# Up products of two feed-forward layers: wide matmuls on high and low parts side by side, then narrow ones

## The chip, the cores and the metric

One core of a Trainium2 chip. The metric is the time of the kernel on the device in microseconds (us), as the median of several runs. All times are for one launch with the inputs of the reference.

## The reference, cut to what matters

A block of a language model, for 512 tokens of width 1024, in float32: a gated feed-forward layer, a mixer (a short convolution and gated linear attention), a second gated feed-forward layer, and a last norm.

```python
def swiglu(x, w_gu, w_down):
    g, u = jnp.split(x @ w_gu, 2, axis=-1)      # 1024 -> 2 x 2816: the "up" products
    return (jax.nn.silu(g) * u) @ w_down        # 2816 -> 1024: the "down" products

x = x + 0.5 * swiglu(rmsnorm(x, norm_ffn1_g), ffn1_w_gu, ffn1_w_down)
x = x + hybrid_mixer(rmsnorm(x, norm_mix_g), ...)
x = x + 0.5 * swiglu(rmsnorm(x, norm_ffn2_g), ffn2_w_gu, ffn2_w_down)
return rmsnorm(x, final_norm_g)
```

## The kernel before, in words

**Layout and precision.** x stands transposed (`X`: 128 partitions, 8 blocks of the width, 512 tokens). A matmul of the kernel takes operands of 128 partitions in the type float32r, which keeps fewer bits than float32. So each operand is split into a high part (ScalarE rounds it: a cast) and a low part (VectorE subtracts the high part), and each product is the sum of three: high by high, high by low, low by high. ScalarE and VectorE split the weights as they arrive (`Weights.issue`, lines 331 and 332: `wh` and `wl`, three buffers each, made up to two products ahead); `Operands.make` (lines 561 and 562) does it for x.

**Sets.** Most of the up products are made in sets by a scheme of seven products in place of eight (as Strassen's): a set makes two column blocks of 256 of the gate and two of the up half, from seven products of sums of weight blocks with sums of x blocks. The products are named m1, p2, q6, p5, q7, p4, p3. The sums of the weights are made by VectorE (line 318, `s3`) and by DMAs that add (line 309, issued on GpSimd's queue); loads are issued on SyncE's queue some steps ahead. The sums of x are made in place (`Operands.sum`, lines 543 to 548), once per layer and during its first set. Each of the seven results goes into one of three accumulators of the set, `a`, `b` or `c`; a PSUM bank holds 512 float32 values a partition, and an accumulator is one bank: two blocks of 128 output columns by 256 tokens. The products of two following sets are interleaved by `order`: ... q6, p5, q7 of a set, m1 of the next, p4, p2 of the next, p3, and then q6 of the next. After the first set m1 is also copied into the next `a` ("fork", line 507).

A product in `Set.run` (line 502) is 24 matmuls, each with its own 128x128 weight tile and 256 columns of x: eight of high weights by high x, eight of high by low x, eight of low by high x. After m1, q6 and q7 ScalarE copies the bank to SBUF (`v`); the rest is done by the function `done` of `up_set` (lines 720 to 745): SiLU of the gate straight from bank `a` after p2, then combinations by VectorE, into the hidden tiles `h`.

**Banks.** There are eight PSUM banks: a pool of six (`MM`) and a pool of two (`AUX`).

**A feed-forward layer** (`ffn`, from line 648): first a "plain" stage without sets for four of the 22 blocks (`mm_group`, `mm_single`, `plain_pair`: VectorE multiplies each bank by the row of the norm, line 476), then nine sets, then the down products: two wide sets of seven products in matmuls of 512 columns (`natural_set`, line 625; `run_wide`), each product in two steps of 12 matmuls, the first three being m1, p5 and q6; then the rest (line 838). In the second layer x has to be turned for the end, since the result leaves with tokens on partitions: `natural(i)` (lines 771 and 772) turns one of eight blocks with four TensorE transposes into an `AUX` bank, and ScalarE copies it back. It is called after p3 of the sets 0 to 7.

Which engine an instruction runs on is fixed in the code. The order of an engine's queue comes from a planner that keeps, by its own estimate of times, to the order of the program where it can and pulls later instructions forward where an engine would be idle.

Of the kernel before, what the change touches and what calls it, by code (L numbers as in the profile page):

```python
# [8 lines left out]
F32 = mybir.dt.float32  # L9
F32R = mybir.dt.float32r  # L10
# [5 lines left out]
P = 128  # L16
# [163 lines left out]
def block_kernel(ctx: ExitStack, tc: tile.TileContext, xT, vecs, gf, gup, wgl, wts, out):  # L180
# [6 lines left out]
    ps = ctx.enter_context(tc.tile_pool(name="ps", bufs=6, space=bass.MemoryType.PSUM))  # L187
    pa = ctx.enter_context(tc.tile_pool(name="pa", bufs=2, space=bass.MemoryType.PSUM))

    cnt = [0]  # L190

# [14 lines left out]
    def T(dtype=F32):  # L206
        return tile_of("tp", [P, S], dtype)

    def MM():
        cnt[0] += 1  # L210
        return ps.tile([P, S], F32, tag="mm", name=f"mm{cnt[0]}")

    def AUX():
        cnt[0] += 1
        return pa.tile([P, S], F32, tag="aux", name=f"aux{cnt[0]}")


    ones = front.tile([P, P], F32, tag="ones", name="ones")
# [260 lines left out]
    class Set:  # L479
# [34 lines left out]
        def first(self):  # L514
# [4 lines left out]
            nc.vector.tensor_tensor(out=t, in0=self.bank["a"], in1=self.v["m1"], op=ALU.add)  # L519
            return t  # L520

    class Operands:

        ORDER = ("m1", "p2", "p5", "q6", "q7", "p4", "p3")

        def __init__(self, b):
            self.b = b
            self.parts = {}  # L530
            self.sums = set()

# [19 lines left out]
        def make(self, p):  # L552
            if p in self.parts:
                return
            i = self.ORDER.index(p)
            if i > 0:
                self.make(self.ORDER[i - 1])
            v = self.sum(p)
            h, l = (tile_of("op", [P, 1024], F32R) for _ in range(2))
            hv, lv = (t.rearrange("p (k t) -> p k t", t=HW) for t in (h, l))  # L560
            nc.scalar.copy(hv, v)
            nc.vector.tensor_tensor(out=lv, in0=v, in1=hv.bitcast(F32), op=ALU.subtract)
            self.parts[p] = (h, l)
# [40 lines left out]
        def get(self, p):  # L604
            return self.parts[p]

    def natural_set(ops, banks, done, ahead=1):

        used = {"a"}
        for at, p in enumerate(SEQ):  # L610
            for q in SEQ[at : at + ahead + 1]:
                ops.make(q)
            n = {"m1": "b", "p2": "a", "q6": "b", "p5": "c", "q7": "b", "p4": "b", "p3": "c"}[p]
            fresh = n not in used
            used.add(n)
            o = banks[n]
            bh, bl = ops.get(p)
            for u in range(2):
                h, l = W.take()
                for j, (ww, aa) in enumerate(((h, bh), (h, bl), (l, bh))):  # L620
                    for i in range(2):
                        k = 2 * u + i
                        for t in range(2):
                            s = slice(k * HW + t * P, k * HW + (t + 1) * P)
                            nc.tensor.matmul(o[t], aa[:, s], ww[:, i * 512 : (i + 1) * 512],  # L625
                                             start=fresh and j == k == 0,
                                             stop=j == 2 and k == 3, skip_group_check=True)
            done(p, o)

    def run_sets(make, ahead=2, hooks={}):  # L630
# [19 lines left out]
    def ffn(up, down, norm, nxt, plain, at):  # L650
        xh, xl = norm.h, norm.l
        rows = []

        def finish(k):
            if k == at:
                rows.append(norm.finish())

        o = mm_group(up, KD, (0, DFF, P, DFF + P), xh, xl, extra=finish, slow=nxt is not None)
        row = rows[0]
        xn, xn_tile = {}, []  # L660

        def normed(j, l):

            if (j, l) not in xn:
                t = slice(l * HW, (l + 1) * HW)
                if not xn:
                    xn_tile.append(tile_of("hidw", [P, 4, 4, HW]))
                v = xn_tile[0][:, len(xn)]
                for i in range(4):
                    k = 4 * j + i  # L670
                    nc.vector.scalar_tensor_tensor(
                        out=v[:, i], in0=x[k][:, t],
                        scalar=vec[:, norm.goff + k : norm.goff + k + 1], in1=row[:, t],
                        op0=ALU.mult, op1=ALU.mult)
                xn[j, l] = v
            return xn[j, l]

        xo = Operands(normed)
# [36 lines left out]

        def down_operands(w):
            return DownOperands(
                lambda j, l: wides[w][:, 4 * j : 4 * j + 4, l * HW : (l + 1) * HW])

        def up_set(i):  # L720
            h = new_hid()

            def done(s, p):
                bank, v = s.bank, s.v
                if p == "p2":
                    s.g1 = T()
                    nc.scalar.activation(s.g1, s.first(), AF.Silu)
                if p == "q7":
                    u2 = T()
                    nc.vector.scalar_tensor_tensor(out=u2, in0=bank["c"], scalar=-1.0, in1=v["q7"],  # L730
                                                   op0=ALU.mult, op1=ALU.subtract)
                    s.u2 = u2
                if p == "p4":
                    nc.vector.scalar_tensor_tensor(
                        out=h[:, :, :HW], in0=pair(bank["b"]), scalar=-1.0, in1=pair(s.g1),
                        op0=ALU.mult, op1=ALU.mult)
                if p == "p3":
                    g2 = T()
                    nc.vector.tensor_tensor(out=g2, in0=bank["c"], in1=v["q6"], op=ALU.add)
# [9 lines left out]
            return Set(xo, done)  # L749

        def pair(t):
            return t.rearrange("p (e t) -> p e t", t=HW)

        run_sets(up_set)

        def split_hid(k):
# [17 lines left out]
    def down_product(us, split_hid, downs, nxt):  # L774
# [26 lines left out]
        A = [MM(), MM()]  # L801

        def run_wide(w):
            banks = {"a": A, "b": [(MM, AUX)[w % 2]() for _ in range(2)], "c": [MM(), MM()]}

            def done(p, o):
                for t in range(2):
# [12 lines left out]

            natural_set(downs[w], banks, done)
            return banks["c"]

        for w in range(WIDE):
            C = run_wide(w)
# [728 lines left out]
```

## Time and profile before

| | |
|---|---|
| median of 3 runs | 1181.12 us (1181.11 to 1181.16) |
| the profiled execution | 1180.99 us, span 1179.3 us |
| TensorE (PE) busy | 1170.9 us, 99% |
| VectorE (DVE) busy | 868.9 us, 74% |
| ScalarE (ACT) busy | 634.3 us, 54% |
| GpSimd (POOL) busy | 117.4 us, 10% |
| matmuls in sets, high weights / low weights | 3584 / 1792 |

A group of instructions is named by its line, engine and operation, and by its output and input (`mm<-op,wh`: into a bank from an operand of x and high weights). Matmuls are pipelined: the busy time of one is longer than the distance to the next, so their distance is read from the start of a run of them and their count. The chain is the work that ended last, followed back from the end, here in order of time: start, length, engine, tile, line, count. In brackets behind an instruction stands how long its engine was idle before it and what released it. In a full queue an instruction starts some 0.1 us before the end that is shown for the one ahead of it.

### The profile page before, as it was taken

How to read it: one execution, taken by the hardware profiler on the slowest of the kernel's cores; microseconds unless marked ns; L12 is line 12 of the kernel's file. 1: busy time of each engine (PE TensorE's matmuls, PEld its weight loads, DVE VectorE, ACT ScalarE, POOL GpSimd, SP SyncE). 2: the span in 40 equal slices, each digit the busy share in tenths (PEclk: the TensorE clock that was granted, in tenths of full speed). 3: DMA queues.
4: the chain of work that ended last, by engine and by line, in shares of the span. 5: the costliest groups of instructions: out<-in, count | busy, mean ns of one | idle time of the engine just before them, and what ended most of it. 6: DMA issues, size and time to landing. Idle time of an engine off the chain costs nothing.

```text
span 1179.3 us, 19168 instructions
## 1 busy us (share of the span) xinstructions
PE 1170.9 (99%) x7794; PEld 1080.7 (92%) x7794; DVE 868.9 (74%) x1027; ACT 634.3 (54%) x790; POOL 117.4 (10%) x153
## 2 busy tenths in 40 slices
PE   9999999999999999999999999999999999999997
PEld 8899999988888889999999998998889999998886
DVE  7985656896568965767697787685598566579955
ACT  6564455674435655565565576544355554566543
POOL 0010101101010111100110100000001111001100
PEclk9999999999999999999999999999999999999999
DMA  9388777678524388777677766531638767757721
GB/s 350 79 210 197 171 193 178 158 199 206 212 85 113 87 207 223 189 180 200 180 196 192 199 199 186 141 109 44 232 68 211 181 180 175 190 153 186 178 83 72
DMA packets 62600, 200.25 MB, mean 170 GB/s; under 512 B 6864, under 2 KB 13136, under 8 KB 62512
## 3 DMA queue, kind: packets, MB, share of 16 engines
q0 software_dynamic: 18784, 68.17, 31.7%
q1 hardware_dynamic: 39088, 126.37, 30.9%
q10 hardware_dynamic: 4640, 4.49, 1.1%
q8 instruction: 61, 1.00, 0.3%
q14 instruction: 27, 0.22, 0.1%
HBM read 124.55 MB, written 8.39 MB: 113 GB/s over the span
## 4 chain that ended last, share of the span: by engine, by line
PE 97%; ACT 1%; issue 1%; DVE 1%; ACTq 0%; POOL 0%; POOLq 0%
PE mm L502 53%; PE mm L625 12%; PE mm L366 11%; PE mm L380 7%; PE mm L838 4%; PE aux L625 4%; PE aux L838 1%; PE aux L1161 1%; PE aux L1142 1%; PE aux L1120 1%; PE aux L1164 0%; PE aux L224 0%; PE aux L1121 0%; PE mm L857 0%; PE aux L771 0%
## 5 line engine op out<-in xcount | busy, mean ns | idle before, releaser
L331 ACT CAST wh<-f 128x1024 fp32r<-128x1024 f32 (+1 forms) x341 | 356.2, 1047 | 406.3 <-PE mm L502 207.4
L332 DVE TENSOR_TENSOR wl<-f,wh 128x1024 fp32r<-128x1024 f32 (+1 forms) x341 | 413.3, 1217 | 154.1 <-ACT wh L331 141.3
L502 PE MATMUL mm<-op,wh 128*128 128x256 f32 x3584 | 471.1, 284 | 0.4 <-ACT mm L507 0.4
L502 PEld LDWEIGHTS mm<-op,wh 128*128 128x128 f32 x3584 | 447.9, 192 | 2.2 <-ACT mm L507 0.8
L502 PE MATMUL mm<-op,wl 128*128 128x256 f32 x1792 | 251.5, 283 | 0.0
L502 PEld LDWEIGHTS mm<-op,wl 128*128 128x128 f32 x1792 | 231.2, 192 | 0.1
L309 POOL DMA_DIRECT2D f<-f x126 | 108.9, 869 | 929.0 <-DVE wl L332 542.2
L625 PE MATMUL mm<-wh,op 128*128 128x512 f32 x432 | 106.9, 389 | 0.0
L625 PEld LDWEIGHTS mm<-wh,op 128*128 128x128 f32 x432 | 80.9, 188 | 16.7
L366 PE MATMUL mm<-op,wh 128*128 128x512 f32 x384 | 91.0, 389 | 0.0
L366 PEld LDWEIGHTS mm<-op,wh 128*128 128x128 f32 x384 | 72.0, 188 | 14.9
L380 PE MATMUL mm<-op,wh 128*128 128x512 f32 x256 | 64.2, 393 | 0.0
L625 PE MATMUL mm<-wl,op 128*128 128x512 f32 x216 | 57.7, 389 | 0.0
L380 PEld LDWEIGHTS mm<-op,wh 128*128 128x128 f32 x256 | 48.1, 189 | 10.3
L318 DVE TENSOR_TENSOR f<-f,f 128x1024 f32<-128x1024 f32 x42 | 51.3, 1222 | 0.8
L625 PEld LDWEIGHTS mm<-wl,op 128*128 128x128 f32 x216 | 40.6, 188 | 8.4
L366 PE MATMUL mm<-op,wl 128*128 128x512 f32 x192 | 47.4, 389 | 0.0
L366 PEld LDWEIGHTS mm<-op,wl 128*128 128x128 f32 x192 | 36.0, 188 | 7.5
L510 ACT COPY tp<-mm 128x512 f32<-128x512 f32 x68 | 39.6, 583 | 0.0
L601 DVE TENSOR_TENSOR op<-hidw,op 128x1024 fp32r<-128x1024 f32 x28 | 34.0, 1219 | 1.1 <-ACT op L600 1.0
L380 PE MATMUL mm<-op,wl 128*128 128x512 f32 x128 | 34.3, 389 | 0.0
L416 ACT ACTIVATE op<-X,vec 128x512 fp32r<-128x512 f32 x23 | 16.5, 719 | 31.8 <-DVE X L859 24.3
(269 smaller groups left out, 1042.5 us busy)
## 6 DMA issues: line engine op xcount, KB each, us to landing
f<-wts SPq DMA_DIRECT2D x219, 512.0 KB, 4.5
f<-f POOLq DMA_DIRECT2D x126, 512.0 KB, 5.3
X<-xT SPq DMA_DIRECT2D x8, 256.0 KB, 5.3
xs<-X POOLq DMA_DIRECT2D x8, 256.0 KB, 2.3
ga<-tp ACTq DMA_DIRECT2D x8, 256.0 KB, 3.2
gb<-tp ACTq DMA_DIRECT2D x8, 256.0 KB, 4.7
tp<-ga SPq DMA_DIRECT2D x8, 256.0 KB, 4.3
y<-tp SPq DMA_DIRECT2D x7, 256.0 KB, 2.3
```

Of the source, the lines that this page charges most:

```text
L309: return nc.gpsimd.dma_start(out_, a, accum_op=ALU.add).ins
L318: nc.vector.tensor_tensor(out=s3, in0=a11, in1=a21, op=ALU.add)
L331: self.cast = nc.scalar.copy(h[:, :w], raw[:, :w]).ins
L332: nc.vector.tensor_tensor(out=l[:, :w], in0=raw[:, :w], in1=h[:, :w].bitcast(F32), op=ALU.subtract)
L366: nc.tensor.matmul(o, w[:, i * P : (i + 1) * P], a[k], start=j == k == 0, stop=j == 2 and k == kt - 1)
L380: nc.tensor.matmul(o[c], w[:, s : s + P], a[k], start=k == 0 and j == 0, stop=k == kt - 1 and j == 2)
L416: nc.scalar.activation(xh[k], x[k], AF.Copy, scale=g)
L502: nc.tensor.matmul(to, ww[:, s], aa[:, t], start=fresh and k == 0 and e == 0 and j == 0, stop=k == 3 and j == 2, skip_group_check=True)
L510: nc.scalar.copy(v, o)
L601: nc.vector.tensor_tensor(out=lv, in0=v, in1=hv.bitcast(F32), op=ALU.subtract)
L625: nc.tensor.matmul(o[t], aa[:, s], ww[:, i * 512 : (i + 1) * 512], start=fresh and j == k == 0, stop=j == 2 and k == 3, skip_group_check=True)
L838: nc.tensor.matmul(o[t][e], b if j == 1 else a, wl if j == 2 else wh, start=k == K0 and e == 1 and j == 0, stop=k == KF - 1 and j == 2, sk ...
```

## The change

1. x's parts of an up product are made by a new class `Both`: two tiles, each with high and low part side by side for two of the four blocks. The split of a product's x is two copies and two subtractions of 512 elements in place of one each of 1024.
2. `PairSet` takes the place of `Set` in `up_set` of both layers (the mixer keeps `Set`). An accumulator is two banks, one for each block of 128 output columns; each has the sums with high x on its left and high by low on its right. A product is eight matmuls of 512 columns (high weights by high and low x), then eight of 256 (low weights by high x, onto the left half). Order of sets and products is as before.
3. Since the result is left plus right, evictions change: `taken` (after m1, q6, q7) is two copies by ScalarE and an addition by VectorE; `whole` is a copy and an addition; `both` is two additions. The fork copies two banks.
4. The eight banks: during the sets one pool with four accumulators of two banks (`w`, `x`, `y`, `z`); `a` is always `x`, and `b` and `c` rotate over the others. The pools of six and two are opened again behind the sets.
5. The eight `natural(i)` of the second layer move from the sets into the first wide set of its down products: two after each of its first two steps, then one after each of the next four. The addition into x after p5 is held until the end of q6.

```diff
+    def banks(paired=False):
+        stage.close()
+        for n, b in (("pairs", 1),) if paired else (("mm", 6), ("aux", 2)):
+            cnt[0] += 1
+            pools[n] = stage.enter_context(tc.tile_pool(
+                name=f"{n}{cnt[0]}", bufs=b, space=bass.MemoryType.PSUM, reuse_waits="tile"))
...
+    def MM2(tag):
+        cnt[0] += 1
+        return pools["pairs"].tile([P, 2, S], F32, tag=tag, name=f"{tag}_{cnt[0]}")
...
+    class Both:
+        def __init__(self, v):
+            self.t = []
+            for i in range(2):
+                t = tile_of("op", [P, 2, 2, HW], F32R)
+                w = v[:, 2 * i : 2 * i + 2]
+                nc.scalar.copy(t[:, :, 0], w)
+                nc.vector.tensor_tensor(out=t[:, :, 1], in0=w, in1=t[:, :, 0].bitcast(F32),
+                                        op=ALU.subtract)
+                self.t.append(t)
...
+    class PairSet:
+        BANK = {"m1": "b", "p2": "a", "q6": "b", "p5": "c", "q7": "b", "p4": "b", "p3": "c"}
+        def __init__(self, group_, done, i):
...
+            self.tags = {"a": "x", "b": "wzy"[i % 3], "c": "ywz"[i % 3]}
...
+        def run(self, p):
+            n = self.BANK[p]
+            fresh = n not in self.bank
+            o = self.open(n) if fresh else self.bank[n]
+            x_ = self.group.get(p)
+            h, l = W.take()
+            for k in range(4):
+                for e in range(2):
+                    nc.tensor.matmul(o[:, e], h[:, k * HW + e * P : k * HW + (e + 1) * P],
+                                     x_.both(k), start=fresh and k == 0, stop=False,
+                                     skip_group_check=True)
+            for k in range(4):
+                for e in range(2):
+                    nc.tensor.matmul(o[:, e, :HW], l[:, k * HW + e * P : k * HW + (e + 1) * P],
+                                     x_.high(k), start=False, stop=k == 3,
+                                     skip_group_check=True)
+            if p == "m1" and self.forked:
+                nc.scalar.copy(self.open("a"), o)
+            elif p in ("m1", "q6", "q7"):
+                self.taken(p, n)
+            self.done(self, p)
+        def taken(self, p, n):
+            v, r = T(), T()
+            nc.scalar.copy(pair(v), self.left(n))
+            nc.scalar.copy(pair(r), self.right(n))
+            nc.vector.tensor_tensor(out=v, in0=v, in1=r, op=ALU.add)
+            setattr(self, p, v)
+        def both(self, n, t):
+            for part in (self.left(n), self.right(n)):
+                nc.vector.tensor_tensor(out=pair(t), in0=part, in1=pair(t), op=ALU.add)
+        def whole(self, n):
+            t = T()
+            nc.scalar.copy(pair(t), self.right(n))
+            nc.vector.tensor_tensor(out=pair(t), in0=self.left(n), in1=pair(t), op=ALU.add)
+            return t
...
             def done(s, p):
-                bank, v = s.bank, s.v
                 if p == "p2":
-                    s.g1 = T()
-                    nc.scalar.activation(s.g1, s.first(), AF.Silu)
+                    if s.forked:
+                        s.g1 = s.whole("a")
+                    else:
+                        s.g1 = s.m1
+                        s.both("a", s.g1)
+                    nc.scalar.activation(s.g1, s.g1, AF.Silu)
                 if p == "q7":
-                    u2 = T()
-                    nc.vector.scalar_tensor_tensor(out=u2, in0=bank["c"], scalar=-1.0, in1=v["q7"],
-                                                   op0=ALU.mult, op1=ALU.subtract)
-                    s.u2 = u2
+                    s.both("c", s.q7)
                 if p == "p4":
+                    t = s.whole("b")
                     nc.vector.scalar_tensor_tensor(
-                        out=h[:, :, :HW], in0=pair(bank["b"]), scalar=-1.0, in1=pair(s.g1),
+                        out=h[:, :, :HW], in0=pair(t), scalar=-1.0, in1=pair(s.g1),
                         op0=ALU.mult, op1=ALU.mult)
                 if p == "p3":
-                    g2 = T()
-                    nc.vector.tensor_tensor(out=g2, in0=bank["c"], in1=v["q6"], op=ALU.add)
-                    nc.scalar.activation(g2, g2, AF.Silu)
-                    mul(h[:, :, HW:], pair(s.u2), pair(g2))
-                    if nxt is None and i < KD:
-                        natural(i)
+                    s.both("c", s.q6)
+                    nc.scalar.activation(s.q6, s.q6, AF.Silu)
+                    nc.vector.scalar_tensor_tensor(
+                        out=h[:, :, HW:], in0=pair(s.q7), scalar=-1.0, in1=pair(s.q6),
+                        op0=ALU.mult, op1=ALU.mult)
...
+        banks(paired=True)
         run_sets(up_set)
+        banks()
...
+            todo = list(range(KD)) if nxt is None and w == 0 else []
+
+            def between():
+                n = 1 + (len(todo) > 4)
+                for i in todo[:n]:
+                    natural(i)
+                del todo[:n]
+
+            natural_set(downs[w], bank, done, between=between)
```

More of the change, by code (lines that the diff above doesn't have):

```diff
@@ L520, in first, with high, both @@
             return t
+    class Both:
[8 more added lines that the diff above has]
+                self.t.append(t)
+        def high(self, k):
+            return self.t[k // 2][:, k % 2, 0]
+        def both(self, k):
+            return self.t[k // 2][:, k % 2].rearrange("p a t -> p (a t)")
@@ new lines, in pair, with left, right, open @@
+    def pair(t):
+        return t.rearrange("p (e t) -> p e t", t=HW)
+    class PairSet:
+        BANK = {"m1": "b", "p2": "a", "q6": "b", "p5": "c", "q7": "b", "p4": "b", "p3": "c"}
+        def __init__(self, group_, done, i):
+            self.group = group_
+            self.done = done
+            self.tags = {"a": "x", "b": "wzy"[i % 3], "c": "ywz"[i % 3]}
+            self.bank = {}
+        def left(self, n):
+            return self.bank[n][:, :, :HW]
+        def right(self, n):
+            return self.bank[n][:, :, HW:]
+        def open(self, n):
+            self.bank[n] = MM2(self.tags[n])
+            return self.bank[n]
+        def run(self, p):
[33 more added lines that the diff above has]
+            return t
@@ L522, in block_kernel, with __init__ @@
     class Operands:
         ORDER = ("m1", "p2", "p5", "q6", "q7", "p4", "p3")
-        def __init__(self, b):
+        def __init__(self, b, kind=None):
             self.b = b
+            self.kind = kind
             self.parts = {}
@@ L558, in make @@
             v = self.sum(p)
+            if self.kind is not None:
+                self.parts[p] = self.kind(v)
+                return
             h, l = (tile_of("op", [P, 1024], F32R) for _ in range(2))
@@ L605, in get, with natural_set @@
             return self.parts[p]
-    def natural_set(ops, banks, done, ahead=1):
+    def natural_set(ops, bank, done, ahead=1, between=None):
         used = {"a"}
@@ L615, in natural_set @@
             used.add(n)
-            o = banks[n]
+            o = bank[n]
             bh, bl = ops.get(p)
@@ L627, in natural_set @@
                                              stop=j == 2 and k == 3, skip_group_check=True)
+                if between is not None:
+                    between()
             done(p, o)
@@ L676, in normed @@
             return xn[j, l]
-        xo = Operands(normed)
+        xo = Operands(normed, Both)
         hid = []
@@ L747, in done @@
                             downs[w].early()
-            return Set(xo, done)
-        def pair(t):
-            return t.rearrange("p (e t) -> p e t", t=HW)
+            return PairSet(xo, done, i)
+        banks(paired=True)
         run_sets(up_set)
+        banks()
         def split_hid(k):
@@ L803, in run_wide @@
         def run_wide(w):
-            banks = {"a": A, "b": [(MM, AUX)[w % 2]() for _ in range(2)], "c": [MM(), MM()]}
+            bank = {"a": A, "b": [(MM, AUX)[w % 2]() for _ in range(2)], "c": [MM(), MM()]}
+            held = []
             def done(p, o):
+                if p == "p5" and nxt is None and w == 0:
+                    held.append(o)
+                    return
+                if held:
+                    for t, o_ in enumerate(held.pop()):
+                        add(1, 1, t, o_, -0.5)
                 for t in range(2):
@@ L819, in done @@
                         add(0, 1, t, o[t], 0.5)
-            natural_set(downs[w], banks, done)
-            return banks["c"]
+            todo = list(range(KD)) if nxt is None and w == 0 else []
[5 more added lines that the diff above has]
+            natural_set(downs[w], bank, done, between=between)
+            return bank["c"]
         for w in range(WIDE):
```

9 lines of the change are left out of this document (5 added, 4 removed).

## The prediction

> **What bounds the kernel now.** I read the page first (engines, slices, clock), then the chain of work that ended last in order of time, then busy time stretch by stretch, and last the instructions of VectorE and ScalarE where those stretches looked full. The profiled execution has a span of 1179.3 us and took 1180.99 us, 0.13 us under the median of the runs, 1181.12; I count from the median.
>
> ```profile
> PE 1170.9 (99%) x7794; PEld 1080.7 (92%) x7794; DVE 868.9 (74%) x1027; ACT 634.3 (54%) x790; POOL 117.4 (10%) x153
> PEclk9999999999999999999999999999999999999999
> ...
> 50.15 181.43 PE mm L502 x1512
> 231.58 38.11 PE mm L625 x168
> 269.69 5.44 PE aux L625 x24
> ...
> 878.47 25.92 PE mm L502 x216
> 904.39 0.44 PE aux L771 x4
> 904.82 20.16 PE mm L502 x168
> ...
> 1046.10 17.27 PE mm L502 x144
> 1063.37 38.11 PE mm L625 x168
> ```
>
> The reader is to see three things. TensorE (PE) is never without work, and its clock is full throughout, so time changes only where its stream gets shorter or gets a hole. The up products of the first feed-forward layer are one unbroken piece of the chain: 1512 matmuls of 256 columns in 181.43 us, 120.0 ns from one to the next (nine sets of 168, 20.16 us a set, 2.88 us a product). And the matmuls of 512 columns (L625, where every one also has its own weight load) run at 38.11/168 = 226.8 ns and 5.44/24 = 226.7 ns. So two narrow matmuls cost 240.0 ns and one wide matmul with as many columns 226.8 ns: each matmul carries about 13 ns that do not depend on its width.
>
> **The stream of TensorE.** A product before is 24 narrow matmuls: high part of the weights by high part of x, high by low, low by high, eight each. The change makes the first sixteen into eight wide ones (high and low of x side by side), and leaves eight narrow. The columns stay the same; 8 matmuls and 8 weight loads go. A product: 8 x 226.8 + 8 x 120.0 = 2.774 us in place of 2.880, so 0.106 us less. Products: 7 in each of 9 sets in each of 2 layers, 126. Gain: 126 x 0.106 = 13.3 us. This is the whole gain, 0.74 us a set. Its two ends: nothing, if the wide matmul among narrow ones costs 240 (no row shows the two kinds mixed in one product); and 13.3, by the rows. I take 13.3, since the narrow stream itself loads a weight tile every 120 ns with the same 13 ns over, so a weight load under a narrow matmul is no worse hidden than under a wide one.
>
> [...]
>
> **What is added beside it: evictions.** High-by-low now lands in a second bank, so each result has to be added up from two. I count by the code, in units of one 128x512 instruction, for a set after the first.
>
> ```profile
> L332 DVE TENSOR_TENSOR wl<-f,wh 128x1024 fp32r<-128x1024 f32 x63 | 76.8, 1222 | 32.8 <-ACT wh L331 31.1 <-DMA f<-wts 1.6
> L331 ACT CAST wh<-f 128x1024 fp32r<-128x1024 f32 x64 | 67.1, 1049 | 81.8 <-PE mm L502 63.1 <-issue 9.4 <-DMA f<-f 8.0
> L510 ACT COPY tp<-mm 128x512 f32<-128x512 f32 x19 | 11.0, 581 | 0.0
> L739 DVE TENSOR_TENSOR tp<-mm,tp 128x512 f32<-128x512 f32 x8 | 5.5, 692 | 10.4 <-PE mm L502 10.4
> L507 ACT COPY mm<-mm 128x512 f32<-128x512 f32 x8 | 4.6, 577 | 0.0
> ...
> 50.15:70.31 20.16, 20.16 (x170) 20.16 (x170) 19.65 (x20) 14.64 (x18) 3.42 (x4) 1.00 0.67 160
> 70.31:90.47 20.16, 20.16 (x170) 20.16 (x170) 14.50 (x15) 10.03 (x13) 3.42 (x4) 1.00 0.92 220
> 110.63:130.79 20.16, 20.16 (x170) 20.16 (x170) 12.20 (x12) 10.02 (x13) 2.57 (x3) 1.00 0.76 183
> 211.43:231.59 20.16, 20.16 (x169) 20.16 (x169) 17.66 (x18) 13.20 (x16) 2.60 (x3) 1.00 0.50 144
> 878.47:899.02 20.55, 20.55 (x174) 20.55 (x173) 20.55 (x22) 14.71 (x18) 3.45 (x4) 1.00 0.69 170
> ```
>
> (The stretches list PE, weight loads, VectorE, ScalarE, GpSimd, then clock, DMA share, GB/s.) VectorE (DVE) before: one at q7, one at p4, two at p3. After: one at q6, three at q7, one at p2, two at p4, three at p3. That is 6 more, at L739's 0.69 us 4.1 us: 12.20 becomes 16.3 us in a set that now lasts 19.4. ScalarE (ACT): one copy more at q6, q7, p2 and p4 (L510, 0.58 each), and the fork copy grows from 512 to 1024 elements; between no more than L507's 0.58 and twice that, I take the cast's 1.05 for the same size: in all 2.8 us, 10.0 becomes 12.8 of 19.4. Both fit. What TensorE waits for inside a set: p2 needs the fork copy, q7 the two copies of q6, p4 those of q7. Always a whole product (2.77 us) lies between. Ahead of them in ScalarE's queue stands one cast, which starts when the high weights are released, two thirds through a product:
>
> ```profile
> 106.82 1.05 ACT L331 CAST wh<-f 128x1024 fp32r<-128x1024 f32 x1 [1.33 <-PE mm L502]
> 107.78 0.57 ACT L507 COPY mm<-mm 128x512 f32<-128x512 f32 x1
> ```
>
> The product ended at 50.15 + 20 x 2.88 = 107.75 and the copy started at 107.78. After the change the high weights are released after 1.81 us of 2.77 (before: 1.92 of 2.88), so the cast ends about 0.2 us after the product, and a copy of 1.05 ends 1.25 into the next one: 1.5 us to spare. So no hole in a set after the first, by these rows. The loads keep their order; the DMA share of 0.76 becomes 0.79, and 0.92 in the second set becomes 0.96, covered by the loads' lead of several products; I cost it at nothing, and if that cover were gone the casts would wait for DMA.
>
> **The first set is where it costs.** There VectorE also makes the operands (sums of x and their low parts), and it was busy 19.65 of 20.16 us, and in the second layer 20.55 of 20.55. Nothing added there is free. The change adds 7 instructions to this set (p2 now takes an addition from both halves, m1 one).
>
> ```profile
> 49.51 0.69 DVE L476 TENSOR_TENSOR tp<-mm,row 128x512 f32<-128x512 f32 x1
> 50.11 1.22 DVE L543 SCALAR_TENSOR_TENSOR hidw<-hidw 128x1024 f32<-128x1024 f32 x1
> 51.24 0.69 DVE L476 TENSOR_TENSOR tp<-mm,row 128x512 f32<-128x512 f32 x1
> ...
> 61.51 1.22 DVE L562 TENSOR_TENSOR op<-hidw,op 128x1024 fp32r<-128x1024 f32 x1
> ...
> 879.53 0.68 DVE L476 TENSOR_TENSOR tp<-mm,row 128x512 f32<-128x512 f32 x1
> 889.27 1.22 DVE L562 TENSOR_TENSOR op<-hidw,op 128x1024 fp32r<-128x1024 f32 x1
> ```
>
> In a full VectorE queue a 128x512 instruction takes 0.60 us (49.51 to 50.11) and a 128x1024 one 1.13 (50.11 to 51.24). The tight place is q7, the fifth product. Its low operand was ready at 61.51 + 1.22 = 62.73; the product began at 50.15 + 4 x 2.88 = 61.67 and first used that operand after eight matmuls, at 62.63. There was no slack at all. Now the low part is needed from the product's first matmul on, at 50.15 + 4 x 2.774 = 61.25, and ahead of it in the queue stand m1's addition and p2's second one (0.60 each), perhaps q6's, and 0.14 for operands made in two pieces: ready at 64.1 to 64.7, a loss of 2.8 to 3.5 us. Part of it comes earlier: the sets now take all eight banks, and if m1 of the first set falls on the banks of the last plain pair, it waits for the read that begins at 51.24 and ends at 51.93, 1.8 us after 50.15. The two do not add, because VectorE catches up while TensorE waits; whichever is later counts. I take 3.0. In the second layer the same operand was ready at 890.49, is now needed at 878.47 + 11.10 = 889.57, and comes 1.3 to 2.0 later than before: 2.2 to 2.9; the bank wait alone (879.53 + 0.68) would be 1.7. I take 2.5. The bounds of this step: nothing, if the additions, which nobody needs soon, are queued behind the operands; and all of the added work in this set, 19.65 + 4.9 - 19.41 = 5.1 and 20.55 + 4.9 - 19.41 = 6.0. With the queue order as it stands, the q7 row is the nearest.
>
> **The way into the down products.**
>
> ```profile
> 214.34 0.69 DVE L739 TENSOR_TENSOR tp<-mm,tp 128x512 f32<-128x512 f32 x1 [1.06 <-PE mm L502]
> 217.38 1.23 DVE L332 TENSOR_TENSOR wl<-f,wh 128x1024 fp32r<-128x1024 f32 x1 [0.62 <-ACT wh L331]
> 225.11 0.69 DVE L730 SCALAR_TENSOR_TENSOR tp<-mm,tp 128x512 f32<-128x512 f32 x1 [0.69 <-ACT tp L510]
> 240.52 2.36 DVE L601 TENSOR_TENSOR op<-hidw,op 128x1024 fp32r<-128x1024 f32 x2 [0.28 <-ACT op L600]
> ...
> 231.00:270.00 39.00, 39.00 (x176) 32.36 (x176) 38.29 (x38) 26.28 (x31) 5.54 (x7) 1.00 0.81 200
> ```
>
> The last set and the down products after it keep VectorE full too (17.66 of 20.16, then 38.29 of 39). In the last set it idles 1.06 + 0.62 + 0.69 = 2.4 us; it gets 6 x 0.60 = 3.6 us more and 0.75 us less time, and one addition more right behind it, so it enters the down products 1.9 to 2.5 us later. The third of them (q6) is the tight one: it began at 231.58 + 4 x 2.72 = 242.46, needed its low operand four matmuls later, at 243.37, and had it at about 241.7, the first of the two at 240.52: slack 1.7. Loss 0.2 to 0.9; between nothing and 2.5 I take 0.9 for the first layer. In the second layer the transposes of x now stand here: eight groups of 0.44 us (the L771 row), the same 3.5 us of TensorE as behind the sets before, so the sum doesn't change, but six groups (2.6 us) fall before q6 and give VectorE that time. Their copies run on ScalarE, 26 of 39 us busy, p5's addition is only held back until x is turned, and the moved step issues no DMA, so no transfer queue sees it. Loss 0.1.
>
> **Sum.** 1181.1 - 13.3 + 3.0 + 2.5 + 0.9 + 0.1 = 1174.3 us. The plain products, the mixer and the tail have no changed instruction; a new order of the queues there I put at nothing, within 1 us either way.
>
> **The rivals.**
> 1. The added work is hidden: VectorE serves operands and low weights before additions, and no bank is waited for. 1181.1 - 13.3 = 1167.8. For it: nearly all the additions have several products until they are needed. Against it: q7's operand had no slack even without them.
> 2. No difference: all the added VectorE work of the first set falls on the path: 13.3 - 5.1 - 6.0 - 1.0 = 1.2 us gained, 1179.9. For it: the 20.55 of 20.55. Against it: the set before ran without a hole although the queue was full, so part of what it held could wait.
> 3. Slower: a wide matmul among narrow ones costs as much as two narrow ones, 240 ns, because its weights load under a narrow one. The gain is gone and the holes stay: 1181.1 + 6.5 = 1187.6. It decides from 226.8 + 6500/1008 = 233.2 ns on. Against it: both pure streams have the same 13 ns. [...]
> 4. Slower by evictions: if reading half of two banks took VectorE twice the 0.60 us, a set would need 7 low weights and one sum at 1.13 and 10 x 1.2, 21.0 us of VectorE against 19.4: 18 x 1.6 = 29 us lost against 13.3 gained, about 1197. It decides at 1.1 us an instruction, where a set is as long as before. Against it: no row shows such a cost; the same view of a bank has not been read before.
>
> **How the numbers follow.** Forecast 0.52 (holes of 4 to 9 us, 1172 to 1177); rival 1 0.22; rival 2, with what lies between it and the forecast, 0.13; rival 3 0.07; rival 4 0.06. A measurement of this kernel can tell about 0.2%, 2.4 us. Below 1178.8 lie forecast, rival 1 and a part of rival 2: 0.80; within 0.2%: 0.07; slower: 0.13. The range goes from rival 1 to rival 2's lower half, 1167.6 to 1179.4.
>
> **What would show it.** Right: in the chain, 16 matmuls a product and 2.77 us from product to product; a set after the first in 19.4 us; VectorE 16.3 and ScalarE 12.8 of it; a hole of up to 2 us before the first product of each layer's sets, named by VectorE's read of a plain product (L476), or before the fifth, named by the operand; the L771 groups between wide down products. Wrong: wide matmuls at 233 ns or over, a hole in every set behind a ScalarE copy, or no hole at all in the first set.

## The result, and the profile after

The changed kernel takes 1187.78 us (median of 4 runs, 1187.47 to 1190.2) against 1181.11: 1.0061 times as long, 95% interval 1.0043 to 1.0078. The forecast was 1174.3, faster; it became 6.7 us slower. The profiled execution took 1187.47 us, span 1185.7.

The page after: TensorE has 1008 matmuls fewer and is busy 4 us less, VectorE 68 us and ScalarE 42 us more; one slice has a lower clock.

```profile
span 1185.7 us, 17379 instructions
PE 1166.8 (98%) x6786; PEld 1029.2 (87%) x6786; DVE 937.2 (79%) x1151; ACT 675.9 (57%) x876; POOL 117.1 (10%) x153
PEclk9999999999999999999999999999999999998999
```

TensorE's queue in order of time, in a middle set of the first layer (wide matmuls line 588, narrow 593):

```profile
116.60 2.00 PE L588 MATMUL w<-op,wh 128*128 128x512 f32 x8
118.44 1.12 PE L593 MATMUL w<-op,wl 128*128 128x256 f32 x8
119.39 2.00 PE L588 MATMUL y<-op,wh 128*128 128x512 f32 x8
```

A product takes 119.39 - 116.60 = 2.79 us; over eight products (116.60 to 138.94) it is 2.793. Eight wide matmuls take 1.84 us, 230 ns each, and eight narrow ones 0.95. So the stream has become shorter, by 0.0875 us a product and 11.0 us in all, and the rest is holes. Three stretches (columns as before: busy PE, weight loads, VectorE, ScalarE, GpSimd, clock, DMA, GB/s): the first set of the first layer, seven products of its middle sets, and the beginning of the wide down products of the second layer.

```profile
50.94:71.91 20.97, 19.85 (x113) 17.27 (x114) 20.97 (x27) 16.24 (x25) 3.42 (x4) 1.00 0.74 170
119.39:138.94 19.55, 19.55 (x114) 17.20 (x113) 15.99 (x18) 12.28 (x17) 2.56 (x3) 1.00 0.76 188
1057.79:1096.79 39.00, 34.30 (x155) 27.68 (x154) 33.20 (x33) 23.72 (x30) 3.18 (x4) 0.91 0.56 137
```

A middle set is as forecast: 19.55 us, TensorE without a hole, VectorE 16.0 and ScalarE 12.3. The first set has VectorE busy every moment. The last row is the loss: 4.7 us without a matmul, clock 0.91. TensorE, ScalarE and VectorE at this place, the entry into the down products of the second layer (L877 are the transposes of x, L878 their copies, L923 the copy of m1, L613 the additions from a bank):

```profile
1061.91 1.06 PE L877 MATMUL aux<-ident,X 128*128 128x128 f32 x8 [1.21 <-DVE tp L613]
1062.73 2.10 PE L729 MATMUL mm<-wh,op 128*128 128x512 f32 x8
1064.67 1.07 PE L729 MATMUL mm<-wl,op 128*128 128x512 f32 x4
1068.14 1.78 PE L877 MATMUL aux<-ident,X 128*128 128x128 f32 x8 [2.40 <-ACT X L878]
1071.01 1.22 PE L729 MATMUL mm<-wh,op 128*128 128x512 f32 x2 [1.08 <-ACT mm L923]
1072.03 1.05 PE L877 MATMUL aux<-ident,X 128*128 128x128 f32 x4
1072.73 3.23 PE L729 MATMUL mm<-wh,op 128*128 128x512 f32 x8
```

```profile
1061.80 0.63 ACT L846 ACTIVATE tp<-tp 128x512 f32<-128x512 f32 x1 [2.72 <-DVE tp L613]
1064.67 1.06 ACT L704 CAST op<-hidw 128x1024 fp32r<-128x1024 f32 x1 [2.24 <-DVE hidw L687]
1065.63 1.03 ACT L346 CAST wh<-f 128x1024 fp32r<-128x1024 f32 x1
1066.57 1.04 ACT L704 CAST op<-hidw 128x1024 fp32r<-128x1024 f32 x1
1067.52 1.06 ACT L878 COPY X<-aux 128x512 f32<-128x512 f32 x2
...
1070.37 0.59 ACT L923 COPY mm<-mm 128x512 f32<-128x512 f32 x1
...
1061.08 0.69 DVE L613 TENSOR_TENSOR tp<-z,tp 128x512 f32<-128x512 f32 x1
1063.41 2.36 DVE L687 SCALAR_TENSOR_TENSOR hidw<-hidw 128x1024 f32<-128x1024 f32 x2
```

Read it downwards. The first transposes write the two banks of accumulator z, which VectorE finishes reading at 1061.08 + 0.69 = 1061.77; TensorE starts them at 1061.91. The second pair needs the first pair's banks back. The transposes were done by 1063.0, but the copy is the fifth instruction in ScalarE's queue, behind a SiLU that waited 2.72 us and a cast that waited 2.24 us, both for VectorE: it starts at 1067.52, and TensorE stands still for 2.40 us. Then m1's copy, queued behind that, is late in its turn (1.08). TensorE is busy for 2.75 of the 5.00 us from 1063 on, and its mean clock in the two stretches behind them is 0.56 and 0.58:

```profile
1063.00:1068.00 5.00, 2.75 (x12) 1.88 (x11) 5.00 (x5) 3.33 (x5) 0.00 (x0) 1.00 0.50 136
1068.00:1071.00 3.00, 1.78 (x8) 1.38 (x8) 2.70 (x4) 3.00 (x6) 0.00 (x0) 0.56 0.59 167
1071.00:1076.00 5.00, 4.99 (x15) 4.08 (x16) 2.14 (x2) 2.97 (x5) 0.00 (x0) 0.58 0.03 8
```

Eight transposes take 1.78 us there in place of 1.06, and eight wide matmuls 3.23 in place of 2.10.

Adding up what the distances of matmul starts have over 226.7 and 120 ns gives the account: the stream 11.0 us shorter; first sets +2.0 (0.7 before the first product, 1.3 before q7) and +1.3; before p4 and p3 of the last sets +1.1 a layer; entry into the down products +1.5 in the first layer and +8.3 in the second; a wait for a copy in the mixer, whose instructions the change leaves alone, +0.7; many small ones, +1.5. Together 6.5 us slower. The 8.3 is read from the length of the stage: from its first matmul at 1057.79 to the first of the rest (L960) at 1145.72 are 87.9 us, against 76.2 before (1063.21 to 1139.40), and 3.5 of the 11.7 between them are no loss, but the eight groups of transposes that stood in the sets before. The two ends before:

```profile
1063.21 2.00 PE L625 MATMUL mm<-wh,op 128*128 128x512 f32 x8
...
1139.40 1.30 PE L838 MATMUL mm<-wh,op 128*128 128x512 f32 x5
```

### The profile page after: what moved, and what is told of

Same layout as the page of the kernel before. It is cut to its first block, busy times and chain, and to the rows that moved or that the text cites. A ratio compares the mean times of both kernels' runs of the same rounds, so it can differ in the third digit from the quotient of the medians.

```text
span 1185.7 us, 17379 instructions
## 1 busy us (share of the span) xinstructions
PE 1166.8 (98%) x6786; PEld 1029.2 (87%) x6786; DVE 937.2 (79%) x1151; ACT 675.9 (57%) x876; POOL 117.1 (10%) x153
## 5 line engine op out<-in xcount | busy, mean ns | idle before, releaser
L517 PE MATMUL mm<-op,wh 128*128 128x256 f32 x1568 | 208.0, 284 | 1.0 <-ACT tp L525 0.6
L517 PEld LDWEIGHTS mm<-op,wh 128*128 128x128 f32 x1568 | 196.9, 191 | 2.7 <-ACT tp L525 0.8
L517 PE MATMUL mm<-op,wl 128*128 128x256 f32 x784 | 110.0, 283 | 0.0
L517 PEld LDWEIGHTS mm<-op,wl 128*128 128x128 f32 x784 | 101.2, 191 | 0.1
L381 PEld LDWEIGHTS mm<-op,wh 128*128 128x128 f32 x384 | 72.0, 188 | 15.0
L588 PE MATMUL w<-op,wh 128*128 128x512 f32 x288 | 72.3, 393 | 2.8 <-DVE op L546 2.3
L588 PE MATMUL z<-op,wh 128*128 128x512 f32 x288 | 72.7, 393 | 1.5 <-DVE tp L613 1.5
L588 PE MATMUL y<-op,wh 128*128 128x512 f32 x288 | 72.3, 393 | 0.1
L588 PEld LDWEIGHTS w<-op,wh 128*128 128x128 f32 x288 | 51.8, 189 | 13.1 <-ACT tp L606 2.9
L588 PEld LDWEIGHTS z<-op,wh 128*128 128x128 f32 x288 | 51.8, 189 | 11.1 <-DVE tp L613 1.9
L588 PEld LDWEIGHTS y<-op,wh 128*128 128x128 f32 x288 | 51.8, 189 | 9.7 <-ACT tp L606 0.5
L395 PEld LDWEIGHTS mm<-op,wh 128*128 128x128 f32 x256 | 48.2, 190 | 10.3
```

What stands on the lines that cost most here:

```text
L381: nc.tensor.matmul(o, w[:, i * P : (i + 1) * P], a[k], start=j == k == 0, stop=j == 2 and k == kt - 1)
L395: nc.tensor.matmul(o[c], w[:, s : s + P], a[k], start=k == 0 and j == 0, stop=k == kt - 1 and j == 2)
L517: nc.tensor.matmul(to, ww[:, s], aa[:, t], start=fresh and k == 0 and e == 0 and j == 0, stop=k == 3 and j == 2, skip_group_check=True)
L588: nc.tensor.matmul(o[:, e], h[:, k * HW + e * P : k * HW + (e + 1) * P], x_.both(k), start=fresh and k == 0, stop=False, skip_group_check= ...
```

## The experiments

Two theories on the entry into the down products of the second layer: Q, the transposes stand behind queues that VectorE holds up; B, VectorE's backlog alone holds the down products up. And E: all the other holes come from the added evictions where VectorE is full.

**The transposes inside the sets again.** Accumulator c of a set is read after its p3 and next written two sets later by m1, so its banks are free in between. (The hold of p5's addition is dropped here too; in the next experiment it stays.)

```diff
-        run_sets(up_set)
+        turn = {} if nxt is not None else {
+            (i + 1, "p5"): [lambda i=i: natural(i, MM2("ywz"[i % 3])[:, 0])] for i in range(KD)}
+        run_sets(up_set, hooks=turn)
...
-            todo = list(range(KD)) if nxt is None and w == 0 else []
+            todo = []
```

> The changed kernel with one thing undone: x of the second layer is turned inside the sets again, behind p5 of the next set, in the two banks of accumulator c that were read before and are next written two products later. Theory Q (queue): the 8 us lost between the sets and the wide down products of the second layer come from the transposes, which stand in TensorE's queue behind a bank that VectorE has still to read and behind copies that ScalarE cannot start because it stands at an instruction waiting for VectorE; half the clock follows. Then the entry costs what it costs in the first layer, 1.5 to 2.5 us: 1181 us (1180 to 1182.5), granted clock 1.00 at the entry. Rival B (backlog): VectorE's backlog of evictions holds the down products back by itself, with or without transposes: 1185 or more, a hole of over 5 us at the same place.

Measured: 1182.72 us, 1.0015 times before (1.0005 to 1.0024). The entry of the second layer:

```profile
1058.03 2.11 PE L588 MATMUL z<-op,wh 128*128 128x512 f32 x8 [0.98 <-DVE tp L613]
1060.92 2.00 PE L729 MATMUL mm<-wh,op 128*128 128x512 f32 x8
...
1060.00:1080.00 20.00, 19.89 (x92) 16.30 (x91) 20.00 (x22) 14.12 (x16) 2.61 (x3) 1.00 0.55 122
```

The 8.3 us became 0.3, with VectorE as full as before (20.00 of 20.00): B is refuted, Q holds. The time is 0.2 us above its range. 2.5 us of holes appeared further on, about 1129 to 1141, most of them behind a cast that waited 5.5 us for a load of weights; why that load was late wasn't pursued.

**The transposes one product later.**

```diff
+            calls = [0]
             def between():
-                n = 1 + (len(todo) > 4)
+                calls[0] += 1
+                n = 2 * (calls[0] > 2)
```

> The changed kernel, but the eight transposes start one product later in the first wide down set: none behind the two steps of m1, two behind each of the four steps of p5 and q6. Theory Q: bank z has been read and ScalarE's queue has moved on by then (5.4 us later), so most of the 5.3 us of holes in front of transposes and of m1's copy go, and the clock stays up: 1181 to 1183 us. Rival B: the hole only moves with them or stays at the operands: 1186 to 1189.

Measured: 1182.30 us, ratio 1.0010 (1.0001 to 1.0019). In the middle of their new place:

```profile
1070.00:1072.00 2.00, 0.71 (x4) 0.25 (x3) 2.00 (x3) 2.00 (x5) 0.00 (x0) 1.00 0.92 256
1072.00:1075.40 3.40, 3.40 (x19) 2.90 (x20) 2.47 (x3) 3.40 (x5) 0.00 (x0) 1.00 0.03 7
1075.40:1077.00 1.60, 0.75 (x5) 0.33 (x5) 1.60 (x3) 1.60 (x3) 0.00 (x0) 1.00 0.00 0
```

Two holes of 1.45 and 1.0 us are left, with full work between them, and the clock stays at 1.00. Two steps of delay are worth 5.5 us.

**The right halves never read.**

```diff
-            v, r = T(), T()
+            v = T()
             nc.scalar.copy(pair(v), self.left(n))
-            nc.scalar.copy(pair(r), self.right(n))
-            nc.vector.tensor_tensor(out=v, in0=v, in1=r, op=ALU.add)
...
-            for part in (self.left(n), self.right(n)):
+            for part in (self.left(n),):
...
-            t = T()
-            nc.scalar.copy(pair(t), self.right(n))
-            nc.vector.tensor_tensor(out=pair(t), in0=self.left(n), in1=pair(t), op=ALU.add)
-            return t
+            return self.left(n)
```

> The changed kernel with the right halves of all accumulators never read: the products of high weights with low x are computed but left out of the result, and each eviction is as many instructions as before the change. TensorE's stream, the banks and the place of the transposes are those of the changed kernel. Theory E with Q: without the added evictions VectorE and ScalarE are not late, the holes go but for the bank wait at the start (0.7): 1181.1 - 11.0 + about 1.5 = 1171.6 us (1170 to 1174). If the transposes cost by their place alone: 1177 to 1179. If the 230 ns of a wide matmul (in place of 226.8) comes from VectorE and ScalarE reading the other banks, a product takes 2.775 in place of 2.793 us and the time is 2 us less still.

Measured: 1173.28 us, ratio 0.9933 (0.9918 to 0.9948). The transposes at the place where the change put them, and a product in a middle set:

```profile
1053.36 1.03 PE L873 MATMUL aux<-ident,X 128*128 128x128 f32 x8
1054.15 2.07 PE L724 MATMUL mm<-wh,op 128*128 128x512 f32 x8
1056.06 1.07 PE L724 MATMUL mm<-wl,op 128*128 128x512 f32 x4
1056.97 1.03 PE L873 MATMUL aux<-ident,X 128*128 128x128 f32 x8
...
120.60 2.00 PE L588 MATMUL w<-op,wh 128*128 128x512 f32 x8
122.44 1.11 PE L593 MATMUL w<-op,wl 128*128 128x256 f32 x8
```

No transpose waits (0.4 us is lost before p5, for m1's copy), and of the holes in the sets only the 0.7 of the first bank and 0.2 before p4 of the second layer's last set are left. So 14.5 us of the changed kernel hang on the added evictions. The wide matmuls still take 230 ns (120.60 to 122.44), so that isn't made by the added reads of the banks.

**Narrow sets where VectorE is full.** `NarrowSet` makes a set as before the change (24 narrow matmuls, an accumulator in one bank, one copy or addition per eviction) on the new operands and banks; transposes as in the first experiment. First and last set of each layer, then each alone, then all nine:

```diff
-            return PairSet(xo, done, i)
+            return (NarrowSet if i in (0, 8) else PairSet)(xo, done, i)   # (0,), (8,), range(9)
```

> Transposes inside the sets as in turn_in_sets, and the first and the last set of each layer made with narrow matmuls and one-bank accumulators as before the change (their evictions too). Theory E (evictions where VectorE is full): 4 x 7 products give back 0.0875 us each, 2.5 us; in return the holes before q7 of the first set (1.3 each), before p2 and p3 of the last set (1.1 each) and at the entry (1.5 each) go: 1176 us (1174.5 to 1178). If those holes have another cause than the added eviction work (the banks, the operands made in two pieces): 1181 + 2.5 = 1183.5.

> turn_in_sets with the first set of each layer alone made narrow. Theory E: the hole before q7 of the first set goes in both layers (1.27 and 1.34), 14 products give back 0.0875 each (1.2): 1182.7 - 2.6 + 1.2 = 1181.3 us (1180.5 to 1182). The holes before p3 of the last set (0.9 and 1.1) and behind it stay. If the first set's crowding delays what follows as well: under 1180.

> turn_in_sets with the last set of each layer alone made narrow. Theory E: the holes before p3 of the last set, at the entry into the wide down products (1.5 in the first layer) and the 2.5 us further on in the second go; 1.2 given back: 1182.7 - 6.2 + 1.2 = 1177.7 us (1176.5 to 1179). The hole before q7 of the first set stays. If the entry is held up by what the sets before the last one left over: 1180 or more.

> turn_in_sets with all nine sets made narrow: the new banks, the operands in two pieces and the new place of the transposes without any wide matmul and without an added eviction. If these parts cost nothing but the wait for the bank at the first set (0.7 in the first layer): 1181.1 + 0.7 = 1181.8 us (1181 to 1182.5), a product in 2.88 us. The difference of narrow_ends to it, over 7 sets, is then the gain of the wide matmuls: 2 x 49 x 0.0875 = 8.6 us by the step measured in the changed kernel, 10.4 by the 0.106 of the prediction.

| sets made narrow | us | ratio to before, 95% |
|---|---|---|
| none | 1182.72 | 1.0015 (1.0005 to 1.0024) |
| first | 1181.86 | 1.0002 (0.9992 to 1.0012) |
| last | 1176.29 | 0.9955 (0.9937 to 0.9973) |
| first and last | 1174.51 | 0.9945 (0.9930 to 0.9960) |
| all nine | 1182.53 | 1.0011 (1.0001 to 1.0020) |

The entry in the first layer with both narrow (last set line 640, down products 765):

```profile
225.70 2.08 PE L640 MATMUL z<-op,wh 128*128 128x256 f32 x16
227.62 1.12 PE L640 MATMUL z<-op,wl 128*128 128x256 f32 x8
228.58 2.00 PE L765 MATMUL mm<-wh,op 128*128 128x512 f32 x8
```

Its last matmuls pass into the down products without a hole, and the holes before q7 of the first sets are gone too; before p4 of the first layer's last set 0.25 us is left. (What the expectations call p2 of the last set is its p4: the product that waits there is the next one to write b.) E holds for the most part: two sets of nine cost more by their evictions than they gain, the last above all. It gives back 6.4 us, which is 0.2 under its range; the first gives back 0.9, or 1.8 where the last is narrow already, which is less than the runs of one kernel here can differ (1182.1 to 1184.79 us with no set narrow). With all nine narrow the kernel is 1.1 us slower than before, 0.7 of it the wait for the first bank: the new banks, operands and place cost nearly nothing by themselves. From all narrow to seven wide sets it is 8.0 us, where 0.0875 us a product gives 8.6. narrow_first gained less than the holes it removed: in the last set of the first layer a hole before p4 grew from 0.2 to 2.0 us. There ScalarE's cast waited for a load of weights, with q7's copies behind it in the queue, so this hole isn't VectorE's doing alone; why the load was later than in the other runs stays open:

```profile
221.71 1.04 ACT L346 CAST wh<-f 128x1024 fp32r<-128x1024 f32 x1 [4.64 <-DMA f<-f]
```

**Wide and narrow matmuls in another order.**

```diff
             for k in range(4):
                 for e in range(2):        # wide: high weights by high and low x
                     ...
-            for k in range(4):
                 for e in range(2):        # narrow: low weights by high x
                     ...
```

> narrow_ends with another order inside a product: for each of four blocks two wide matmuls and then two narrow ones, in place of eight wide and then eight narrow. Theory S (switch): the wide matmuls right behind narrow ones are the slow ones (233 to 236 ns, then 226.7), so four switches a product in place of one cost more: a product 2.80 to 2.86 in place of 2.793 us, in all 98 products 1 to 6 us. Rival: wide matmuls in a mixed stream cost 230 ns anyway, or the order helps: 2.78 to 2.80, no difference.

Measured: 1173.30 us, ratio 0.9932 (0.9916 to 0.9948), the fastest of the complete kernels, 8.1 us under before in its own comparison.

```profile
121.15 0.63 PE L591 MATMUL w<-op,wh 128*128 128x512 f32 x2
121.62 0.39 PE L595 MATMUL w<-op,wl 128*128 128x256 f32 x2
121.84 0.63 PE L591 MATMUL w<-op,wh 128*128 128x512 f32 x2
...
123.93 0.63 PE L591 MATMUL z<-op,wh 128*128 128x512 f32 x2
```

A product takes 123.934 - 121.148 = 2.786 us, not more than 2.793 as theory S said: S fell. The two wide matmuls of a group take 463 to 469 ns, slower than 453, but the two narrow ones only 228 to 233 in place of 240.

**Hardly any narrow matmuls.**

```diff
-            for k in range(4):
-                for e in range(2):
-                    nc.tensor.matmul(o[:, e, :HW], l[:, k * HW + e * P : k * HW + (e + 1) * P],
-                                     x_.high(k), start=False, stop=k == 3, ...)
+            nc.tensor.matmul(o[:, 0, :HW], l[:, :P], x_.high(0), start=False, stop=True, ...)
```

> narrow_ends with seven of the eight narrow matmuls of a wide product left out (low weights by high x, so the result lacks them). Its time says little, since the other engines then set the pace; what is read is the distance of the eight wide matmuls of a product. If wide matmuls are slowed by narrow ones near them, they run at 226.7 to 228 ns, the first one or two excepted. If it is something of their own (two banks in turn, x's parts as they lie), they stay at 230 and over, five of eight at 231 to 236.

```profile
153.81 1.98 PE L591 MATMUL z<-op,wh 128*128 128x512 f32 x8
155.62 0.28 PE L594 MATMUL z<-op,wl 128*128 128x256 f32 x1
155.73 0.40 PE L591 MATMUL w<-op,wh 128*128 128x512 f32 x1
155.97 0.40 PE L591 MATMUL y<-op,wh 128*128 128x512 f32 x1
```

The eight at 153.81, with wide ones ahead of them, take 1.81 us, 226.6 each. In the product at 155.73, behind one narrow matmul, the first two take 232 and 236 again (the next starts at 155.97). So the same wide matmuls run at 226.6 ns behind wide ones, and the slow ones are the five behind a narrow one (233, 236, 228, 233 and 231 ns in the changed kernel at 119.39), about 27 ns together. (The kernel ran once, at 1136.02 us; only the distances are read.) The changed kernel shows nearly the same behind a hole between wide matmuls alone, in the down products of the first layer: of the eight at 238.59 the second to fifth take 236, 228, 233 and 231 ns. So in both places it stands at the start of a run of wide matmuls, behind narrow ones as behind a hole; what makes it stays open.

**Accumulator x on the first banks.**

```diff
         banks(paired=True)
+        MM2("x")
```

> mixed_order with accumulator x laid on the first two banks, so that m1 of the first set no longer falls on the banks of the last plain pair. If the 0.7 us hole at the first set comes from VectorE's late read of that bank, it goes: 1173.3 - 0.7 = 1172.6 us. If TensorE would have waited for an operand or the weights at that place anyway, or the hole moves to p2: 1173.3.

Measured: 1175.25 us, ratio 0.9951 (0.9937 to 0.9964): no gain, and 1.9 us more than mixed_order, where 0.7 less or no difference was expected. The 0.7 us before the first set of the first layer went, and one of 1.7 came before that of the second:

```profile
872.68 1.97 PE L381 MATMUL mm<-op,wl 128*128 128x512 f32 x8
876.18 2.15 PE L639 MATMUL w<-op,wh 128*128 128x256 f32 x16 [1.53 <-ACT op L545]
...
875.35 0.68 DVE L491 TENSOR_TENSOR tp<-mm,row 128x512 f32<-128x512 f32 x1
```

The trace names an operand's cast; VectorE's read of the last plain bank ends 0.15 us before the start, which fits the same wait on the other layer's banks. Which of them it is wasn't told apart.

## Why the prediction was wrong

The step that failed is "The way into the down products", second layer: "Loss 0.1". It measured 8.3 us. I had counted the 2.6 us of transposes as time given to VectorE, and their copies by ScalarE's share of the stage, "26 of 39 us busy". That share says nothing of the place in the queue: ScalarE stood at instructions that waited for VectorE, so copies that nothing else held back came 4.5 us late. And I had not asked who reads the banks that the transposes are given: those of z, the last that the last set frees. Moved into a stage where VectorE was full, a step without a VectorE instruction took on VectorE's lateness. turn_in_sets and turn_later each give back 5 us, and left_only takes all but 1.1 us of it away with the transposes where they are.

The other steps:
- The stream: 13.3 us forecast, 11.0 measured. The mis-sized term is the wide matmul, 226.8 forecast, 230 measured, because the narrow ones cut the wide ones into runs of eight, and the first five of a run are slow (228 to 236 ns at 119.39; in wide_only eight that follow wide ones take 226.6 each). The 11.0 us are 10.9 ns for each of the 1008 matmuls that went, where the forecast had 13.
- The first sets: 3.0 and 2.5 forecast, 2.0 and 1.3 measured. The mechanism was right, place and all: before the first product a wait for L491, before q7 one for the operand's low part (L546). What I left out is that the operand now comes in two pieces, and q7 can start on the first of them.
- The last sets: 1.1 us a layer before p4 and p3, not forecast; I had argued with middle sets alone. There p3 writes c again two products after VectorE is free to read it, where a middle set has three, and VectorE was late. (The set before the last has two as well, and no hole.) Ahead of that stands a load, and the loads I had put at nothing: ScalarE's cast waited 2.81 us for one (1.45 at the same place before the change), q7's copies stood behind it, and the additions from c (L613) came after them. The second layer has the same row, with 2.82. The added evictions are part of it, since with the last set alone made narrow the cast waited 3.35 us in the first layer and no hole was left there; in the second layer a hole of 1.4 us before p4 stayed.

```profile
220.86 1.05 ACT L346 CAST wh<-f 128x1024 fp32r<-128x1024 f32 x1 [2.81 <-DMA f<-f]
226.75 2.11 PE L588 MATMUL z<-op,wh 128*128 128x512 f32 x8 [0.76 <-DVE tp L613]
```

- The entry in the first layer: 0.9 forecast, 1.5 measured, but not by the step that was forecast. One hole stands before p5's second step, for high weights that ScalarE cast late, and one before q6, for m1's copy; no wait names q6's low operand. It is the queue of the second layer again, without transposes: a SiLU and a cast ahead had waited 2.73 and 2.23 us for VectorE.

```profile
238.59 2.11 PE L729 MATMUL mm<-wh,op 128*128 128x512 f32 x8 [0.59 <-ACT wh L346]
```

- Middle sets: no hole, VectorE 16.0 and ScalarE 12.3 us, as forecast (16.3 and 12.8).
- The rivals: the time landed on that of rival 3 (1187.6) by chance, since wide matmuls at 230 are under its 233. Rival 1, all added work hidden, gave 1167.8; even with the added evictions left out (left_only) it is 1173.28. None of the three signs of being wrong that the prediction names appeared: they watch the stream and the sets, and the loss came behind the sets.

## What to carry to other kernels

Fewer matmuls with the same columns were worth 11.0 us here, 10.9 ns each; what was paid for them is the second bank to read (14.5 us hang on it, left_only), and where VectorE was already full that price lay on the path. Make such a change only in the stages where VectorE has room: seven of nine sets gave 7 to 8 us, all nine gave none. Before moving a step, look past its engine's share of the stage: which instructions stand ahead of it in each queue, what they wait for, and who is the last reader of the buffers that it takes.

## What the runs showed of the hardware

In the changed kernel TensorE's clock was at 0.50 for 6.8 us, from 1068.39 to 1075.21 (the means of 0.56 and 0.58 above). The longest hole ahead of it is the 2.40 us before the second transposes; TensorE had been busy 2.75 of the 5.00 us to 1068. Wide matmuls and transposes took about twice their time in part of that stretch, some 2.5 us in all (1.2 and 0.6 on ten wide matmuls, 0.7 on eight transposes). In wide_only the clock was at half for 3.4 us behind one hole of 2.9 us (the second row gives the clock, 0.50, behind GpSimd's busy time):

```profile
992.65 0.66 PE L637 MATMUL y<-op,wh 128*128 128x256 f32 x3 [2.93 <-ACT wh L346]
993.10:996.50 3.40, 3.40 (x10) 2.65 (x9) 2.50 (x3) 0.46 (x1) 0.00 (x0) 0.50 0.02 5
```

Holes of 1.45 and 1.0 us with 3.4 us of full work between them (turn_later) left the clock at 1.00. So in these three stretches it was at half behind holes of 2.40 and 2.93 us and full behind 1.45 and 1.0. What decides isn't shown, nor whether the hole of 1.21 us ahead of the one of 2.40 had a part in it.

In the changed kernel, of the wide matmuls that follow a narrow one the first five take 233, 236, 228, 233 and 231 ns (the product at 119.39), until 226.7 is reached; the first narrow one behind wide ones takes 113 to 117 in place of 120.
